# The norm factor at the opening of a second feed-forward: tokens on partitions, copied banks, and later state steps

## The chip, the core and the metric

The kernel runs on one core of a Trainium2 chip. A core has five engines, each with its own instruction queue, worked through in order: TensorE (PE in the profile; PEld is its loading of the stationary operand), VectorE (DVE), ScalarE (ACT), GpSimd (POOL) and SyncE (SP). Engines wait for one another on semaphores. Data lies in SBUF, 128 partitions wide; TensorE writes its products to PSUM, which has eight banks of 128 x 512 f32 values. The metric is the time of one execution on the device in microseconds (us), as the median of several runs.

## The reference, cut to what matters

One step of a decoder block on 512 prompt tokens and 8 sample tokens, 520 in all, with 1024 features: a feed-forward with half weight, a mixer (causal pooling heads and state-space heads), a second feed-forward with half weight, and a last norm.

```python
def _rms_norm(x, g):
    xf = x.astype(jnp.float32)
    y = xf * lax.rsqrt(jnp.mean(xf * xf, axis=-1, keepdims=True) + EPS)
    return (y * g.astype(jnp.float32)).astype(x.dtype)

def _swiglu(x, wg, wu, wd):
    return (jax.nn.silu(x @ wg) * (x @ wu)) @ wd
...
        h = h + m
        h = h + 0.5 * _swiglu(_rms_norm(h, ffn2_norm[l]), ffn2_w_gate[l], ffn2_w_up[l], ffn2_w_down[l])
```

The norm's factor is one number for each token. The kernel multiplies the products of gate and up by it, after the matrix products, since a factor of a token can be taken out of a sum over features. The mixer also gives back new recurrent states; for the 8 sample tokens each is `decay * state + x * dt * B`, 1024 rows of 128 values for each token.

## The kernel before, in words

Features lie on partitions, tokens along the free dimension, in two halves of 260 columns (`HALVES`, `HB`). The hidden width of 2816 is 22 tiles of 128. A feed-forward goes through them in groups of 6, 6, 6 and 4 (`CHUNKS`), the first group in the order 0, 3, 1, 4, 2, 5 (`order`).

Most products use a scheme with seven products in place of eight (`product`, numbers 1 to 7), each of them three products of f32 values split into a high and a low part (`mm3`, L124 to L128). Of one tile, four products add into the bank `A` (1, 6, 7, 4) and three into the pair of banks `BE` (5, 3, 2). Between the products into `A`, ScalarE copies what the bank holds to `ac` (L444). PSUM has two slots for `A`, two for `BE` (a pair each) and two single banks `ps`.

Tile 0 of the second feed-forward is different: it is computed plainly in f32 (`plain`, L317) while the mixer's last output products still run, and its gate and its up part each hold one pair of `BE`. It opens the feed-forward:

- `scales` calls `rstds` and `rstd`: TensorE multiplies the sums of squares `acc` (128 partitions x 520 tokens) by a matrix of ones, so that each partition gets the sum for every token (L171, two products of 260 columns); ScalarE takes the root out of PSUM (L172), VectorE the reciprocal (L173). The factor `r` then stands on all 128 partitions.
- `plain_out(0)` multiplies the gate's banks by `r` (VectorE, L355, two halves), applies Silu (ScalarE, L357), multiplies by `r` again (L358), and multiplies by the up part's banks (L360, two halves). L355 and L360 free the two pairs of `BE`.
- `behind`: the weights of the third tile in the order (tile 1) are prepared on VectorE only behind L355's last instruction.

Then `rest` calls `step` for each tile. Each step also calls `state` twice (or more in the last group, `catch_up`), which moves the new states of the sample tokens on by one piece: a generator of 32 items with two pieces each. An item loads rows by GpSimd's queue (L1018, L1024), scales them by four ScalarE instructions (L1044, L1045), adds them on VectorE (L1046) and stores them (L1028). Loads, scalings and stores are pinned behind what was written before them on their engine. `at_border` names the steps that leave it out. What is left at the end is run in one go before the last product of the last tile, ahead of the down products of the last group.

The order of instructions in each engine's queue is otherwise made by a planner at build time, from priorities and its own estimate of each instruction's time; `high_priority` puts a block first, and what one place of the program changes can change the order of what follows.

Of the kernel before, what the change touches and what calls it, by code (L numbers as in the profile page):

```python
# [9 lines left out]
F32 = mybir.dt.float32  # L10
F32R = mybir.dt.float32r
AF = mybir.ActivationFunctionType
ALU = mybir.AluOpType
# [3 lines left out]
P = 128  # L17
D = 1024
# [3 lines left out]
HB = NT // 2  # L22
HALVES = (slice(0, HB), slice(HB, NT))
# [38 lines left out]
def tile_trunk_step(ctx: ExitStack, tc: tile.TileContext, ins: dict, outs: dict):  # L62
    nc = tc.nc
# [20 lines left out]

    ones = cst.tile([P, P], F32, tag="ones", name="ones")
    nc.vector.memset(ones, 1.0)
    eps = cst.tile([P, 1], F32, tag="eps", name="eps")
    nc.vector.memset(eps, EPS)

# [40 lines left out]
    def ws(w, k, m=P):  # L130
        return w[:, k * m : (k + 1) * m]
# [77 lines left out]
    class Ffn:  # L209
# [3 lines left out]

        def __init__(self, nx, i, wx, gp, direct):
            self.nx, self.i, self.wx, self.gp, self.direct = nx, i, wx, gp, direct
            self.states = self.pending = self.gx = None
            self.w, self.A, self.BE, self.ac, self.g, self.tg, self.raw, self.banks, self.behind = ({} for _ in range(9))
            self.out, self.gt, self.early, self.added = {}, {}, {}, {}
            self.chunk, self.chunks, lo = {}, [], 0
            for c, n in enumerate(CHUNKS):  # L220
                fs = list(range(lo, lo + n))
                if c < PAIRED:
                    fs = [lo + q * (n // 2) + k for k in range(n // 2) for q in range(2)]
                self.chunks.append(fs)
                self.chunk.update({f: c for f in fs})
                lo += n
            self.order = [f for fs in self.chunks for f in fs]
# [77 lines left out]
        def plain(self, f, xg, j, us=(0, 1)):  # L305
            for u in us:
                if (f, u) not in self.banks:
                    n = f"P{self.i}_{f}{u}"
                    if f and u == 0:
                        bs = [ps[0].tile([P, 512], F32, tag="A", bufs=2, name=f"{n}{b}") for b in range(2)]  # L310
                    else:
                        t = ps[0].tile([P, 2, 512], F32, tag="BE", bufs=2, name=n)
                        bs = [t[:, 0], t[:, 1]]
                    self.banks[f, u] = bs
                for q in range(2):
                    for b, slot in enumerate(((0, 1), (3, 2))):
                        nc.tensor.matmul(self.banks[f, u][b][:, :HB], ws(self.raw[f][:, u], j + 4 * q), xg[:, slot[q]],  # L317
                                         start=j == q == 0, stop=j == 3 and q == 1, skip_group_check=True)
# [11 lines left out]
        def plain_mixed(self, f, xgs):  # L330
# [9 lines left out]
            for low in (False, True):  # L340
                for u in range(2):
                    w = self.w[f, u][low]
                    for j in range(n):
                        for q, b in ((0, 0), (1, 0), (1, 1)):
                            for x in (xth,) if low else (xth, xtl):
                                nc.tensor.matmul(self.banks[f, u][b][:, :HB], ws(w, j + 4 * q), x[:, j, q + b],
                                                 start=not low and x is xth and j == q == 0,
                                                 stop=low and j == n - 1 and q == 1, skip_group_check=True)

        def plain_out(self, f):  # L350
            tg = self.wx.tile([P, 2, HB], F32, tag="tg", bufs=2, name=f"tg{self.i}_{f}")
            self.tg[f] = tg
            self.g_homes(f)
            for b, hs in enumerate(HALVES):
                free = nc.vector.tensor_tensor(out=tg[:, b], in0=self.banks[f, 0][b][:, :HB], in1=self.nx[3][:, hs],  # L355
                                               op=ALU.mult)
            nc.scalar.activation(out=tg, in_=tg, func=AF.Silu)  # L357
            nc.vector.tensor_tensor(out=tg, in0=tg, in1=self.halves(self.nx[3]), op=ALU.mult)  # L358
            for b in range(2):
                nc.vector.scalar_tensor_tensor(out=self.out[f][:, b], in0=self.banks[f, 1][b][:, :HB],  # L360
                                               scalar=0.5, in1=tg[:, b], op0=ALU.mult, op1=ALU.mult)
            self.g_split(f)
            return free.ins

# [113 lines left out]
        def close(self, k):  # L478
# [4 lines left out]
            with self.first_if(k):  # L483
                self.up(k, 0, self.A[k][:, :HB])
                self.g_split(k, True)

        def scales(self):
            return rstds(self.nx, f"f{self.i}")

# [43 lines left out]
        def at_border(self, k):  # L533
            if isinstance(k, tuple):
                return k[1] in (0, 2)
            return self.chunk[k] < PAIRED and k == self.chunks[self.chunk[k]][-1]

        def state(self, k):
# [129 lines left out]
    f2 = {}  # L668
# [29 lines left out]
    f2["ffn"].states = f2["states"](f2["st"])  # L698
    next(f2["ffn"].states)
    with tc.high_priority():  # L700
        f2["ffn"].scales()
        f2["ffn"].behind[f2["ffn"].order[2]] = f2["ffn"].plain_out(0)

    res = []
# [58 lines left out]
def mixer(tc, ins, outs, e):  # L763
    nc = tc.nc
    cst, act, wp, tmp, dr, pool = (e[x] for x in ("cst", "act", "wp", "tmp", "dr", "pool"))
    ones = e["ones"]
    bank, load_unit, mm3, ws, v, rstd, rstds, vec, h, nx2, raw_tile, open_f2, fin, fill = (
        e[x] for x in ("bank", "load_unit", "mm3", "ws", "v", "rstd", "rstds", "vec", "h", "nx2", "raw_tile",
                       "open_f2", "fin", "fill"))
    xh, xl, _, r = nx2[0]  # L770
    xa = e["xa"][0]
    mp = pool("mx", "right")

    ident = cst.tile([P, P], F32, tag="ident", name="ident")
    nc.sync.dma_start(out=ident, in_=ins["ident"])
    tri = cst.tile([P, P], F32, tag="tri", name="tri")
    nc.sync.dma_start(out=tri, in_=ins["tri"])
# [544 lines left out]
```

## Time and profile before

| | |
|---|---|
| median of 3 runs | 972.12 us (971.78 to 979.32) |
| profiled execution | 970.42 us |
| its span, first to last instruction | 968.7 us |
| TensorE busy | 942.4 us, 97% |
| VectorE busy | 859.2 us, 89% |
| ScalarE busy | 694.3 us, 72% |
| GpSimd busy | 232.1 us, 24% |
| mean granted TensorE clock | 0.997 of full speed |

Times in the views count from the first instruction. A row of a timeline has start, duration, engine, line, operation, the tile written and those read, shapes and count; a bracket behind it holds the engine's idle time just before and what ended it. A row of groups has busy time and mean duration in ns, and then idle time. A row of a line's view has the shortest, the median and the longest duration in ns. A row of stretches has the length, then for PE, PEld, DVE, ACT and POOL the busy time and the number of instructions, then the granted clock, the share of DMA and GB/s. The second feed-forward's own products begin at about 619 us, and its last product ends just before 960 us.

### The profile page before, as it was taken

The numbers are of one execution on the slowest core, as the hardware profiler recorded it, in microseconds if no ns is written. First come the engines' busy times: TensorE is split into PE (matmuls) and PEld (weight loads), VectorE is DVE, ScalarE is ACT, GpSimd is POOL, SyncE is SP. The second block draws the span as 40 slices with busy tenths as digits, with TensorE's granted clock in tenths as the row PEclk, the third lists the DMA queues.
The fourth block names the chain that finished last, engine by engine and source line by source line (L and its number), as shares of the span: only waits on it lengthen the run. The fifth ranks groups of instructions, "written<-read, shape, count | busy, mean of one in ns | idle before, by whom it ended". The sixth has DMA issues, their size and how long they took to land.

```text
span 968.7 us, 20265 instructions
## 1 busy us (share of the span) xinstructions
PE 942.4 (97%) x7636; PEld 922.2 (95%) x7636; DVE 859.2 (89%) x1616; ACT 694.3 (72%) x1293; POOL 232.1 (24%) x341
## 2 busy tenths in 40 slices
PE   7999999999999999999999999999999999999995
PEld 6999999999999999989899999899999999999995
DVE  7999899989999698688989876999989999999986
ACT  8777677667767475686776556687788778887984
POOL 0111211121122000156523111122142223323430
PEclk9999999999999999999999999999999999999998
DMA  7565775675666243264598777466587668767852
GB/s 243 149 174 119 180 178 126 149 188 146 157 148 170 68 151 119 80 189 120 165 261 221 168 178 160 120 155 155 139 219 184 169 152 218 184 149 188 202 155 89
DMA packets 66739, 157.01 MB, mean 162 GB/s; under 512 B 9608, under 2 KB 22856, under 8 KB 66640
## 3 DMA queue, kind: packets, MB, share of 16 engines
q1 hardware_dynamic: 41168, 103.78, 34.0%
q0 software_dynamic: 25472, 51.92, 29.0%
q8 instruction: 60, 0.98, 0.4%
q14 instruction: 39, 0.32, 0.1%
HBM read 148.33 MB, written 7.34 MB: 161 GB/s over the span
## 4 chain that ended last, share of the span: by engine, by line
PE 86%; DVE 6%; DMA 3%; ACT 3%; issue 2%; POOL 0%; SPq 0%; DVEq 0%; ACTq 0%
PE A L128 8%; PE A L124 8%; PE A L127 8%; PE BE L128 6%; PE BE L124 6%; PE BE L127 6%; PE P L317 3%; PE wo L124 2%; PE wo L128 2%; PE wo L127 2%; PE A2d L127 2%; PE A2d L124 2%; PE A2d L128 2%; PE inz L124 2%; PE A1d L128 2%
## 5 line engine op out<-in xcount | busy, mean ns | idle before, releaser
L444 ACT COPY ac<-A 128x260 f32<-128x260 f32 x123 | 45.5, 370 | 17.0 <-PE A L128 16.6
L387 DVE TENSOR_TENSOR s<-raw 128x1024 f32<-128x1024 f32 x41 | 49.9, 1217 | 3.4 <-DMA raw<-in_w1gu 2.7
L124 PE MATMUL inz<-xh_mx,whi_inz 128*128 128x260 f32 x128 | 36.8, 287 | 1.0 <-DVE E L1122 1.0
L317 PE MATMUL P<-xg_f,raw 128*128 128x260 f32 x128 | 32.5, 407 | 5.3 <-DMA raw<-in_w1gu 5.3
L124 PE MATMUL wo<-catg,whi_wo 128*128 128x260 f32 x128 | 37.2, 290 | 0.0
L124 PE MATMUL inx<-xh_mx,whi_inx 128*128 128x260 f32 x128 | 36.4, 285 | 0.0
L128 PE MATMUL wo<-catg,wlo_wo 128*128 128x260 f32 x128 | 36.2, 283 | 0.0
L128 PE MATMUL inz<-xh_mx,wlo_inz 128*128 128x260 f32 x128 | 36.2, 283 | 0.0
L128 PE MATMUL inx<-xh_mx,wlo_inx 128*128 128x260 f32 x128 | 36.2, 283 | 0.0
L127 PE MATMUL inx<-xl_mx,whi_inx 128*128 128x260 f32 x128 | 36.1, 282 | 0.0
L127 PE MATMUL inz<-xl_mx,whi_inz 128*128 128x260 f32 x128 | 36.1, 282 | 0.0
L127 PE MATMUL wo<-catg,whi_wo 128*128 128x260 f32 x128 | 36.1, 282 | 0.0
L1028 POOL DMA_DIRECT2D out_nss<-hs x32 | 22.0, 688 | 52.1 <-DVE hs L1046 52.1
L317 PEld LDWEIGHTS P<-xg_f,raw 128*128 128x128 f32 x128 | 25.5, 204 | 9.2 <-ACT xg_f L193 5.2
L892 DVE SCALAR_TENSOR_TENSOR A<-U,h,A 128x544 f32<-128x544 f32 x36 | 28.1, 781 | 4.9 <-ACT A L890 4.6
L456 DVE TENSOR_TENSOR tg<-BE,ac 128x520 f32<-128x520 f32 x41 | 28.4, 693 | 2.8 <-PE BE L128 2.8
L466 DVE TENSOR_TENSOR tg<-tg,r_f 128x520 f32<-128x520 f32 x41 | 28.5, 695 | 2.7 <-ACT tg L464 2.6
L1146 DVE TENSOR_TENSOR h<-wo,h 128x260 f32<-128x260 f32 x48 | 19.4, 417 | 12.7 <-PE wo L128 12.7
L107 ACT CAST whi_wo<-raw_wo 128x1024 fp32r<-128x1024 f32 x12 | 12.6, 1046 | 24.7 <-issue 16.3
L998 DVE SCALAR_TENSOR_TENSOR junk<-h,cb 128x128 f32<-128x128 f32 x64 | 21.9, 343 | 9.1 <-DMA cb<-scr_bc 8.1
L464 ACT ACTIVATE tg<-tg 128x520 f32<-128x520 f32 x41 | 26.2, 639 | 3.9 <-DVE tg L463 3.9
L463 DVE TENSOR_TENSOR tg<-tg,r_f 128x520 f32<-128x520 f32 x41 | 28.4, 693 | 0.1
(1802 smaller groups left out, 4810.5 us busy)
## 6 DMA issues: line engine op xcount, KB each, us to landing
raw<-in_w2gu SPq DMA_DIRECT2D x44, 512.0 KB, 4.8
raw<-in_w1gu SPq DMA_DIRECT2D x42, 512.0 KB, 4.6
raw_1d<-in_w1d SPq DMA_DIRECT2D x24, 384.0 KB, 4.0
raw_2d<-in_w2d SPq DMA_DIRECT2D x24, 384.0 KB, 3.9
raw_wo<-in_w_out SPq DMA_DIRECT2D x12, 512.0 KB, 6.6
wlo_wo<-in_w_out POOLq DMA_DIRECT2D x12, 512.0 KB, 7.7
ab<-scr_acs SPq DMA_DIRECT2D x8, 512.0 KB, 5.7
h<-in_state_ssm SPq DMA_DIRECT2D x16, 256.0 KB, 7.4
```

Source lines behind the costliest of these rows:

```text
L124: first = nc.tensor.matmul(ps, whi, xhi, start=start, stop=False, **kw)
L127: nc.tensor.matmul(ps, whi, xlo, start=False, stop=False, **kw)
L128: nc.tensor.matmul(ps, wlo, xhi, start=False, stop=stop, **kw)
L317: nc.tensor.matmul(self.banks[f, u][b][:, :HB], ws(self.raw[f][:, u], j + 4 * q), xg[:, slot[q]], start=j == q == 0, stop=j == 3 and q == ...
L387: nc.vector.tensor_tensor(out=s1, in0=diag, in1=up0, op=ALU.add)
L444: nc.scalar.copy(keep, out[:, :HB])
L456: nc.vector.tensor_tensor(out=tg, in0=self.BE[k][:, :, :HB], in1=a, op=ALU.add)
L463: nc.vector.tensor_tensor(out=tg, in0=tg, in1=r, op=ALU.mult)
L464: nc.scalar.activation(out=tg, in_=tg, func=AF.Silu)
L466: nc.vector.tensor_tensor(out=tg, in0=tg, in1=r, op=ALU.mult)
L892: nc.vector.scalar_tensor_tensor(out=A[:, :n], in0=U[:, j : j + n], scalar=w(j), in1=A[:, :n], op0=ALU.mult, op1=ALU.add)
L1028: pin(nc.gpsimd.dma_start(out=js(outs["nss"], i), in_=t))
```

## The change

Three things change at the opening of the second feed-forward; the first feed-forward is left as it was.

1. The factor: `turned_scales` replaces `scales`. Eight products with 65 tokens of `acc` as the stationary operand and two columns of ones as the moving one put the sums on 65 partitions, 16 columns in all. Root and reciprocal work on that 65 x 16 block. Eight more products, with one column of the result spread over 128 stationary columns and a 65 x 65 identity moving, put each factor on all 128 partitions, in two banks; ScalarE copies these to `r`.
2. The plain tile: `plain_free` copies the gate's pair of banks to `tg` on ScalarE, ahead of the factor; `plain_out` copies the up pair to its home on ScalarE. The multiplications then work in SBUF, each as one instruction of 520 columns.
3. The states: `at_border` leaves out the second and third tile of the order (tiles 3 and 1).

The tile `ident` is allocated at the program's start; it is loaded where it was.

```diff
+        def gate_home(self, f):
+            if f not in self.tg:
+                self.tg[f] = self.wx.tile([P, 2, HB], F32, tag="tg", bufs=2, name=f"tg{self.i}_{f}")
+            return self.tg[f]
+
+        def plain_free(self, f):
+            nc.scalar.copy(self.gate_home(f), self.pairs[f][0][:, :, :HB])
+
         def plain_out(self, f):
-            tg = self.wx.tile([P, 2, HB], F32, tag="tg", bufs=2, name=f"tg{self.i}_{f}")
-            self.tg[f] = tg
+            tg = self.gate_home(f)
             self.g_homes(f)
-            for b, hs in enumerate(HALVES):
-                free = nc.vector.tensor_tensor(out=tg[:, b], in0=self.banks[f, 0][b][:, :HB], in1=self.nx[3][:, hs],
-                                               op=ALU.mult)
+            out, r = self.out[f], self.halves(self.nx[3])
+            if f in self.pairs:
+                nc.scalar.copy(out, self.pairs[f][1][:, :, :HB])
+                free = nc.vector.tensor_tensor(out=tg, in0=tg, in1=r, op=ALU.mult)
...
             nc.scalar.activation(out=tg, in_=tg, func=AF.Silu)
-            nc.vector.tensor_tensor(out=tg, in0=tg, in1=self.halves(self.nx[3]), op=ALU.mult)
-            for b in range(2):
-                nc.vector.scalar_tensor_tensor(out=self.out[f][:, b], in0=self.banks[f, 1][b][:, :HB],
-                                               scalar=0.5, in1=tg[:, b], op0=ALU.mult, op1=ALU.mult)
+            nc.vector.tensor_tensor(out=tg, in0=tg, in1=r, op=ALU.mult)
+            if f in self.pairs:
+                nc.vector.scalar_tensor_tensor(out=out, in0=out, scalar=0.5, in1=tg, op0=ALU.mult, op1=ALU.mult)
...
+        def turned_scales(self):
+            acc, r = self.nx[2:]
+            n, q = HB // 4, 2
+            ps = bank("psr_t")
+            for j in range(8):
+                nc.tensor.matmul(ps[:n, q * j : q * j + q], acc[:, n * j : n * j + n], ones[:, :q], start=True, stop=True,
+                                 skip_group_check=True)
+            rt = tmp.tile([P, HB], F32, tag="ta", name="rt")[:n, : 8 * q]
+            nc.scalar.activation(out=rt, in_=ps[:n, : 8 * q], func=AF.Sqrt, bias=eps[:n], scale=1.0 / D)
+            nc.vector.reciprocal(out=rt, in_=rt)
+            for b, hs in enumerate(HALVES):
+                pr = bank(f"pr_t{b}")
+                for j in range(4):
+                    c = rt[:, q * (4 * b + j) : q * (4 * b + j) + 1]
+                    nc.tensor.matmul(pr[:, n * j : n * j + n], c.to_broadcast([n, P]), ident[:n, :n], start=True,
+                                     stop=True, skip_group_check=True)
+                nc.scalar.copy(r[:, hs], pr[:, :HB])
...
         def at_border(self, k):
             if isinstance(k, tuple):
                 return k[1] in (0, 2)
+            if k in self.order[1:3]:
+                return True
             return self.chunk[k] < PAIRED and k == self.chunks[self.chunk[k]][-1]
...
     with tc.high_priority():
-        f2["ffn"].scales()
+        f2["ffn"].plain_free(0)
+        f2["ffn"].turned_scales()
         f2["ffn"].behind[f2["ffn"].order[2]] = f2["ffn"].plain_out(0)
```

More of the change, by code (lines that the diff above doesn't have):

```diff
@@ L86, in tile_trunk_step @@
     nc.vector.memset(ones, 1.0)
+    ident = cst.tile([P, P], F32, tag="ident", name="ident")
     eps = cst.tile([P, 1], F32, tag="eps", name="eps")
@@ L215, in __init__ @@
             self.nx, self.i, self.wx, self.gp, self.direct = nx, i, wx, gp, direct
+            self.pairs = {}
             self.states = self.pending = self.gx = None
@@ L313, in plain @@
                         bs = [t[:, 0], t[:, 1]]
+                        if self.i == 2:
+                            self.pairs.setdefault(f, []).append(t)
                     self.banks[f, u] = bs
@@ L348, in plain_mixed @@
                                                  stop=low and j == n - 1 and q == 1, skip_group_check=True)
+        def gate_home(self, f):
[4 more added lines that the diff above has]
+            nc.scalar.copy(self.gate_home(f), self.pairs[f][0][:, :, :HB])
         def plain_out(self, f):
-            tg = self.wx.tile([P, 2, HB], F32, tag="tg", bufs=2, name=f"tg{self.i}_{f}")
-            self.tg[f] = tg
+            tg = self.gate_home(f)
             self.g_homes(f)
-            for b, hs in enumerate(HALVES):
-                free = nc.vector.tensor_tensor(out=tg[:, b], in0=self.banks[f, 0][b][:, :HB], in1=self.nx[3][:, hs],
-                                               op=ALU.mult)
-            nc.scalar.activation(out=tg, in_=tg, func=AF.Silu)
-            nc.vector.tensor_tensor(out=tg, in0=tg, in1=self.halves(self.nx[3]), op=ALU.mult)
-            for b in range(2):
-                nc.vector.scalar_tensor_tensor(out=self.out[f][:, b], in0=self.banks[f, 1][b][:, :HB],
-                                               scalar=0.5, in1=tg[:, b], op0=ALU.mult, op1=ALU.mult)
+            out, r = self.out[f], self.halves(self.nx[3])
+            if f in self.pairs:
+                nc.scalar.copy(out, self.pairs[f][1][:, :, :HB])
+                free = nc.vector.tensor_tensor(out=tg, in0=tg, in1=r, op=ALU.mult)
+            else:
+                for b, hs in enumerate(HALVES):
+                    free = nc.vector.tensor_tensor(out=tg[:, b], in0=self.banks[f, 0][b][:, :HB],
+                                                   in1=self.nx[3][:, hs], op=ALU.mult)
+            nc.scalar.activation(out=tg, in_=tg, func=AF.Silu)
+            nc.vector.tensor_tensor(out=tg, in0=tg, in1=r, op=ALU.mult)
+            if f in self.pairs:
+                nc.vector.scalar_tensor_tensor(out=out, in0=out, scalar=0.5, in1=tg, op0=ALU.mult, op1=ALU.mult)
+            else:
+                for b in range(2):
+                    nc.vector.scalar_tensor_tensor(out=out[:, b], in0=self.banks[f, 1][b][:, :HB],
+                                                   scalar=0.5, in1=tg[:, b], op0=ALU.mult, op1=ALU.mult)
             self.g_split(f)
@@ L485, in close @@
                 self.g_split(k, True)
+        def turned_scales(self):
[8 more added lines that the diff above has]
+            nc.vector.reciprocal(out=rt, in_=rt)
+            for b, hs in enumerate(HALVES):
+                pr = bank(f"pr_t{b}")
[4 more added lines that the diff above has]
+                nc.scalar.copy(r[:, hs], pr[:, :HB])
         def scales(self):
@@ L772, in mixer @@
     mp = pool("mx", "right")
-    ident = cst.tile([P, P], F32, tag="ident", name="ident")
+    ident = e["ident"]
     nc.sync.dma_start(out=ident, in_=ins["ident"])
```

## The prediction

> **What bounds the kernel now.** I read the page first: the shares of the engines, then the chain that ended last.
>
> ```profile
> span 968.7 us, 20265 instructions
> PE 942.4 (97%) x7636; PEld 922.2 (95%) x7636; DVE 859.2 (89%) x1616; ACT 694.3 (72%) x1293; POOL 232.1 (24%) x341
> PE 86%; DVE 6%; DMA 3%; ACT 3%; issue 2%; POOL 0%; SPq 0%; DVEq 0%; ACTq 0%
> ```
>
> TensorE is busy 97% of the span and is 86% of the chain. All its idle time together is 968.7 - 942.4 = 26.3 us. So a change can gain only what it takes off TensorE's own work, plus idle time of TensorE that it closes; work given to or taken from VectorE counts only where TensorE waits for it. That makes the place of the change the next view: the timeline of TensorE from the last products of the plain tile on. An entry in brackets is idle time just before a row, with what ended it.
>
> ```profile
> 621.56 1.04 PE L171 MATMUL psr_f<-acc_f,ones 128*128 128x260 f32 x4
> 622.25 0.48 PE L124 MATMUL A<-xth_f,whi_3a 128*128 128x260 f32 x1
> 622.56 0.28 PE L127 MATMUL A<-xtl_f,whi_3a 128*128 128x260 f32 x1
> 622.68 0.28 PE L128 MATMUL A<-xth_f,wlo_3a 128*128 128x260 f32 x1
> 623.50 0.38 PE L124 MATMUL A<-xth_f,shi_3d 128*128 128x260 f32 x1 [0.54 <-ACT ac L444]
> ...
> 625.66 0.39 PE L124 MATMUL A<-xth_f,shi_3c 128*128 128x260 f32 x1 [0.47 <-ACT ac L444]
> ...
> 627.83 0.39 PE L124 MATMUL A<-xth_f,whi_3b 128*128 128x260 f32 x1 [0.47 <-ACT ac L444]
> ...
> 633.21 0.39 PE L124 MATMUL BE<-xth_f,shi_3d 128*128 128x260 f32 x1 [1.02 <-ACT ac L444]
> ...
> 637.99 0.39 PE L128 MATMUL A<-xth_f,slo_1d 128*128 128x260 f32 x1
> ...
> 659.01 0.39 PE L124 MATMUL BE<-xth_f,shi_2d 128*128 128x260 f32 x1 [0.38 <-ACT ac L444]
> ...
> 659.76 0.38 PE L128 MATMUL A<-xth_f,slo_2d 128*128 128x260 f32 x1 [0.25 <-DVE slo_2d L115]
> ```
>
> Tile 3 runs four groups of products into the one bank A, one after another, and before each of three of them waits for ScalarE to copy A away; a fourth wait is for a copy of BE. The four waits are 0.54 + 0.47 + 0.47 + 1.02 = 2.50 us. They are there because BE has only two pairs of banks and both still hold the plain tile, whose release hangs on the norm factor. Why that is late shows on VectorE and ScalarE:
>
> ```profile
> 623.63 3.41 DVE L173 RECIPROCAL r_f<-r_f 128x260 f32<-128x260 f32 x2
> 626.95 0.70 DVE L355 TENSOR_TENSOR tg<-P,r_f 128x260 f32<-128x260 f32 x2
> ...
> 630.94 0.70 DVE L358 TENSOR_TENSOR tg<-tg,r_f 128x520 f32<-128x520 f32 x1 [1.22 <-ACT tg L357]
> ...
> 632.16 0.76 DVE L360 SCALAR_TENSOR_TENSOR gx<-P,tg 128x260 f32<-128x260 f32 x2
> ```
> ```profile
> 622.34 0.84 ACT L172 ACTIVATE r_f<-psr_f,eps 128x260 f32<-128x260 f32 x2
> ...
> 627.67 0.40 ACT L1044 ACTIVATE hs<-hs,sdec 128x128 f32<-128x128 f32 x1
> ...
> 628.97 1.28 ACT L357 ACT_TABLE_LOAD   x1
> 630.27 0.64 ACT L357 ACTIVATE tg<-tg 128x520 f32<-128x520 f32 x1
> ```
>
> Two reciprocals of 3.41 us stand before L355 frees the gate's banks (627.65), and L360 frees the up half's only at 632.92. Between them the states' four scalings (627.67 on) push the table load and the Silu back, and VectorE waits 1.22 us.
>
> **The change, part by part.** First, the products that are added. The rows nearest to them are these, with the start of what follows:
>
> ```profile
> 435.11 1.09 PE L1112 MATMUL yd<-ab,xdt 128*64 128x128 f32 x16
> 436.13 0.39 PE L124 MATMUL inp<-xh_mx,whi_inp 128*128 128x260 f32 x1
> 436.36 0.28 PE L127 MATMUL inp<-xl_mx,whi_inp 128*128 128x260 f32 x1
> ...
> 370.97 1.20 PE L839 MATMUL psdv<-sel,dv 48*128 48x16 f32 x10
> 372.10 0.39 PE L124 MATMUL inbc<-xh_mx,whi_inbc 128*128 128x260 f32 x1
> ```
>
> A plain f32 product is two records (the two products of the old factor are the x4 of L171). With 64 stationary columns a record takes (436.13 - 435.11) / 16 = 0.064 us, with 128 columns and 16 moving ones (372.10 - 370.97) / 10 = 0.113 us, so the load of the stationary side sets the pace, not the moving side. The new sums are 8 products with 65 stationary columns and 2 moving: 16 records, 1.0 us by the row with 64 columns, at most 1.8 us by the other; I take 1.0. The spreading is 8 products with 128 stationary columns and 65 rows: 16 records, 1.8 us by the psdv row, at least 1.0 us; I take 1.8. The old two products leave: from 621.56 to about 622.44 (the row at 622.25 reaches its successor 0.31 us later where the pace is 0.12), 0.88 us. Coming back from f32 products costs TensorE 0.23 - 0.12 = 0.11 us at 436.13; the spreading can stand apart from the sums in one piece or two, 0.1 to 0.2 us; I take 0.2. Together 1.0 + 1.8 + 0.2 - 0.9 = **+2.1 us of TensorE work**, between 2.0 + 0.1 - 0.9 = +1.2 and 3.6 + 0.2 - 0.9 = +2.9. Nothing covers it while TensorE is the bound.
>
> [...]
>
> Second, the copies that free the banks. Two ScalarE copies of 128x520 out of the banks are added. The nearest rows are the copy of half the size and the Silu of the full size:
>
> ```profile
> L444 ACT COPY ac<-A 128x260 f32<-128x260 f32 x5 | 1.9, 375 | 4.0 <-PE A L128 4.0
> L357 ACT ACTIVATE tg<-tg 128x520 f32<-128x520 f32 x1 | 0.6, 638 | 0.0
> ```
>
> So 0.64 each (0.75 as two halves). The first can start when the plain tile's products end, near 621.7, and needs no norm factor; the second needs the slot of the sum of squares, which is free once the new sums are made, near 622.6. So the gate's pair is free about 622.4 and the up pair about 623.4, instead of 627.65 and 632.92. Tile 3 can then run in its written order, A and BE in turn, and each copy of A lies beside 12 products of another bank (12 x 0.12 = 1.4 us against 0.37). I cost this **-2.5 us**, between 0 and -2.5. ScalarE gets two copies (1.3), two more of 128x260 for the factor (0.75) and one small root; it loses the two roots (0.84). Between 618 and 640, the stretch of these rows, it sat idle 4.0 us waiting for A alone.
>
> Third, VectorE: the 3.41 us of reciprocals become one of 65x16. Nearest are a small operation of either engine:
>
> ```profile
> L854 DVE TENSOR_SCALAR dt_e<-dt_q x1: 201/201/201, 379.5 to 379.5; 128x80 f32<-128x80 f32 x1
> L1076 ACT ACTIVATE we<-we x8: 190/206/209, 418.8 to 507.9; 128x8 f32<-128x8 f32 x8
> ```
>
> 0.2 us each. But VectorE can use little of the 3.2 us: the preparation of tile 1 is queued on it behind the product that L355 makes (`behind`), and that now waits for sums (1.0), root, reciprocal, spreading (1.8) and two copies. From 621.56: 1.0 + 0.4 + 0.3 + 1.8 + 0.5 gives a factor at about 625.8 and the product done at 626.6, against 627.65. What it frees is 1.0 us there, and with the states gone the Silu follows at once, which removes the 1.22 us wait and one addition of 0.42 us: tile 1's last operand (637.99) would be ready some 2 us earlier, and TensorE arrives there at nearly the old time. Of the three small waits later (0.1 at 637.99, 0.38, 0.25) I let 0.3 go: **-0.3**, between 0 and -0.75.
>
> Fourth, the states. Two of the 32 items (two steps each for tiles 3 and 1) move to the end, ahead of the last product of tile 21. That is 8 scalings, 2 additions and the loads, one row and stores of POOL's queue. There the profile shows:
>
> ```profile
> 930.00:940.00 10.00, 9.99 (x83) 9.78 (x82) 8.22 (x16) 8.26 (x22) 3.23 (x6) 1.00 0.59 184
> 940.00:950.00 10.00, 10.00 (x86) 10.00 (x85) 8.30 (x21) 7.98 (x22) 0.55 (x1) 1.00 0.03 14
> ...
> 937.61 0.62 ACT L249 CAST gt<-tg 128x520 fp32r<-128x520 f32 x1
> ...
> 938.65 0.40 ACT L1044 ACTIVATE hs<-hs,sdec 128x128 f32<-128x128 f32 x1
> ...
> 940.68 0.55 POOL L1028 DMA_DIRECT2D out_nss<-hs  x1 [3.44 <-DVE hs L1046]
> ```
>
> An item is 4 scalings, from 938.65 to the next cast at 939.84, 1.2 us of ScalarE. Two are 2.4 us, and the twenty microseconds shown leave ScalarE 3.8 us idle, while TensorE runs on through the down products. I cost it 0; without that cover, see the third rival.
>
> **The sum.** +2.1 - 2.5 - 0.3 + 0 = -0.7 us. The profiled execution took 970.42 us (its span of 968.7 and 1.7 around it), so 969.7; the median of the runs shown is 972.12, 1.7 above it, so I forecast **971.4 us**.
>
> **The rivals.** *Slower, TensorE waits for its own factor.* TensorE takes its instructions in order. If the spreading is queued close behind the sums, it waits for drain (0.28 less the pace of 0.12), root, reciprocal and three hand-overs: 0.2 + 0.4 + 0.2 + 3 x 0.1 = 1.1 us (a hand-over: the product at 622.68 ends 622.96 and ScalarE's copy starts 623.07), and 1.2 more if the reciprocal meets one of VectorE's 1.2 us operations. It decides from the point where fewer than about ten products of tile 3 stand between. For it: the old factor was placed with only the plain tile's products before it and had priority; against it: tile 3's operands are ready and could fill the gap. 971.4 + 2.3 = 973.7 us.
>
> *Cheaper products.* The loads hide behind running products: the pace is then that of the moving side, 0.22 us for 260 columns (0.88 / 4), so 0.055 for 65 and next to nothing for 2: 16 x 0.055 = 0.9 instead of 2.8. 971.4 - 1.9 = 969.5 us. [...]
>
> *The tail.* The moved states are pinned in order. Each waits for a load:
>
> ```profile
> L1018 POOL DMA_DIRECT2D hs<-in_state_ssm x32: 538/568/899, 621.3 to 934.1; - x32
> DMA to landing us min/median/max: 2.3/3.9/6.9
> ```
>
> If two items stand ahead of the last tile's cast (937.61), ScalarE is held for 2 x 3.9 us, and TensorE's cover is 27 products of the first three outputs, 3.2 us: 4.6 us late, 971.4 + 4.6 less what ScalarE does meanwhile, about 975. For it: the last items already ran beside the down products; against it: the cast has priority.
>
> *It doesn't do what it says.* The banks are held anyway, by the next tile's operands or by the queue order: the stalls stay and the work is paid, 971.4 + 2.8 = 974.2 us.
>
> **How the numbers follow.** Chances: forecast 0.45 (own range 970.1 to 972.5: 1.2 - 2.5 - 0.75 = -2.05 and 2.9 - 2.5 = +0.4 by the ends of the terms, the stall closed), waits for the factor 0.22, cheaper products 0.12, tail 0.12, no earlier banks 0.06, and 0.03 that the planner's new order costs or gains more anywhere in the 340 us behind. The range 968.8 to 975.6 reaches from below the cheaper products to the tail. One per cent, 9.7 us, is about what a measurement of this kernel tells from no change. No case but the last reaches it: faster 0.02, within 0.94, slower 0.04.
>
> **What would show it.** Right: records of the sums near 0.065 us and of the spreading near 0.11; no row of tile 3 in TensorE's timeline that waits for a copy of A; BE written right after the first group of A; the Silu straight behind its product. Wrong: an idle entry before the spreading that names the reciprocal or the root; new waits for ScalarE's copies, now that four more stand in its queue; idle time of TensorE between 930 and 945. The forecast falls too if the new order opens wider waits at the later borders between groups of tiles, of which this is one today:
>
> ```profile
> PE BE2d L124 <- ACT shi_2d_0c L107: 0.9, 1, 0.9
> ```

## The result, and the profile after

The changed kernel takes 979.18 us (median of 22 runs, 973.07 to 985.49), the kernel before, run beside it, 975.73 us (22 runs, 969.72 to 980.74). The medians differ by 3.4 us; the ratio of the runs, estimated with its 95% interval, is 1.0051 (1.0031 to 1.0071): slower by half a per cent, 5.0 us, where no change to speak of was forecast. Its profiled execution took 976.3 us. The page of the changed kernel begins so (engines, then the shares of the chain that ended last):

```profile
span 974.5 us, 20318 instructions
PE 945.7 (97%) x7664; PEld 925.5 (95%) x7664; DVE 855.3 (88%) x1613; ACT 695.3 (71%) x1296; POOL 232.2 (24%) x341
PE 80%; DVE 7%; DMA 7%; ACT 3%; issue 2%; POOL 1%; SPq 0%; DVEq 0%; ACTq 0%; POOLq 0%
```

TensorE's idle time is now 974.5 - 945.7 = 28.8 us against 26.3, and it is busy 3.3 us longer. To see where, I cut the span on TensorE at three instructions that both kernels have: the first product for the norm factor's sums; the first product with `shi_2d_0c` (685.38 before, 688.47 after); and the first with `whi_21a` (920.03 and 923.12). **Opening**, **middle** and **tail** are the stretches from each to the next, the tail up to the span's end.

| | sums start at | opening | middle | tail |
|---|---|---|---|---|
| before | 621.56 | 63.82 | 234.65 | 48.67 |
| after | 622.99 | 65.48 | 234.65 | 51.38 |
| difference | 1.43 | 1.66 | 0.00 | 2.71 |

Ahead of the opening TensorE's records show the same instructions in the same order, but for a few records that either trace lacks, so I put the 1.43 us there down to the execution, not to the change. In a second profile of the changed kernel (e6) the sums start at 623.43, and in a kernel that differs from the one before only in its states (e9) at 625.29. The change costs 1.66 us where it is made and 2.71 us at the end: 4.4 us in this pair of profiles, beside 5.0 us in the timed runs.

TensorE's timeline of the opening after the change (start, duration, instruction, idle time before it in brackets):

```profile
622.99 1.05 PE L511 MATMUL psr_t<-ones,acc_f 128*65 128x2 f32 x16
623.90 0.37 PE L125 MATMUL A<-xth_f,whi_3a 128*128 128x260 f32 x1
624.11 0.28 PE L125 MATMUL BE<-xth_f,shi_3c 128*128 128x260 f32 x1
...
626.05 0.39 PE L125 MATMUL A<-xth_f,shi_3d 128*128 128x260 f32 x1
...
627.59 1.90 PE L520 MATMUL pr_t<-ident,rt 65*128 65x65 f32 x16
629.29 0.37 PE L125 MATMUL BE<-xth_f,shi_3d 128*128 128x260 f32 x1
...
639.05 0.39 PE L125 MATMUL A<-xth_f,shi_1d 128*128 128x260 f32 x1 [1.04 <-ACT shi_1d L108]
...
641.10 0.41 PE L129 MATMUL A<-xth_f,slo_1d 128*128 128x260 f32 x1 [1.27 <-DVE slo_1d L116]
...
641.51 0.42 PE L128 MATMUL A<-xtl_f,shi_1d 128*128 128x260 f32 x1
641.73 0.42 PE L129 MATMUL A<-xth_f,slo_1d 128*128 128x260 f32 x1
...
644.76 0.29 PE L125 MATMUL BE<-xth_f,shi_1d 128*128 128x260 f32 x1
```

The sums take 623.90 - 622.99 = 0.91 us, the spreading 629.29 - 627.59 = 1.70. `BE` is written straight behind the first products into `A`, and no row of tile 3 has an idle entry; only the one at 626.05 starts 0.39 us behind the row before it, where the pace is 0.12, just as ScalarE's copy of `A` ends (626.00). But tile 1 now waits twice, 1.04 + 1.27 us, nearly as long as the four waits that went. And behind those waits a product starts 0.22 us after the last one (641.51, 641.73) where the pace elsewhere is 0.12. The view of stretches says why (length, busy time and count for PE, PEld, DVE, ACT, POOL, granted clock, DMA share, GB/s):

```profile
638.00:641.20 3.20, 0.89 (x6) 0.68 (x5) 3.20 (x5) 1.81 (x4) 0.86 (x1) 1.00 0.88 221
641.20:644.80 3.60, 3.60 (x18) 3.60 (x19) 3.39 (x8) 0.90 (x2) 0.00 (x0) 0.53 0.75 197
644.80:648.00 3.20, 3.20 (x28) 3.20 (x28) 2.32 (x4) 2.42 (x4) 0.00 (x0) 1.00 0.00 0
```

In 3.2 us TensorE was busy for 0.89; in the 3.6 us that follow its granted clock is 0.53. Why the operands of tile 1 are late shows on VectorE, where they are prepared, and on ScalarE. VectorE after the change:

```profile
625.05 0.24 DVE L515 RECIPROCAL rt<-rt 65x16 f32<-65x16 f32 x1
629.93 0.70 DVE L368 TENSOR_TENSOR tg<-tg,r_f 128x520 f32<-128x520 f32 x1 [4.64 <-ACT r_f L522]
...
639.82 1.22 DVE L116 TENSOR_TENSOR slo_1d<-s,shi_1d 128x1024 fp32r<-128x1024 f32 x1
```

ScalarE after the change:

```profile
629.52 0.38 ACT L522 COPY r_f<-pr_t 128x260 f32<-128x260 f32 x1 [0.52 <-PE pr_t L520]
629.92 1.28 ACT L373 ACT_TABLE_LOAD   x1
631.21 0.64 ACT L373 ACTIVATE tg<-tg 128x520 f32<-128x520 f32 x1
...
636.48 1.05 ACT L108 CAST whi_4a<-raw 128x1024 fp32r<-128x1024 f32 x1 [0.93 <-PE A L128]
637.43 0.63 ACT L112 ACTIVATE wlo_4a<-raw 128x512 fp32r<-128x512 f32 x1
637.97 1.03 ACT L108 CAST shi_1d<-s 128x1024 fp32r<-128x1024 f32 x1
```

The reciprocal starts 0.70 us behind the end of the root, since VectorE is still at work on another operation (L208, 1.24 us from 623.89), and is done at 625.29. But TensorE spreads it only at 627.59, behind three groups of tile 3, where the planner has put it. VectorE, in order, stands idle for 4.64 us before L368, and everything for tile 1 is queued behind L368. On ScalarE the casts of tile 4 then stand ahead of that of `shi_1d`.

The tail, TensorE after the change:

```profile
938.46 0.39 PE L125 MATMUL dh<-gt,shi_2d 128*128 128x260 f32 x1 [0.42 <-ACT shi_2d L108]
...
957.95 0.60 PE L780 MATMUL psl<-acc_last,ones 128*128 128x260 f32 x2
...
960.66 0.60 PE L780 MATMUL psl<-acc_last,ones 128*128 128x260 f32 x2
962.42 0.71 PE L780 MATMUL psl<-sq_last,ones 128*128 128x260 f32 x2 [1.16 <-ACT sq_last L764]
963.57 0.71 PE L780 MATMUL psl<-sq_last,ones 128*128 128x260 f32 x2 [0.44 <-ACT sq_last L764]
```

and before it:

```profile
951.00 0.60 PE L740 MATMUL psl<-acc_last,ones 128*128 128x260 f32 x2
...
956.70 0.60 PE L740 MATMUL psl<-acc_last,ones 128*128 128x260 f32 x2
957.42 0.71 PE L740 MATMUL psl<-sq_last,ones 128*128 128x260 f32 x2
```

`psl` is the last norm's sum, one for each half of the tokens. Before, the first half's stood 5.70 us ahead of the second's, and its root and reciprocals ran beside TensorE's last down products. After, it stands 2.71 us ahead. TensorE waits for nothing there; only its place in the queue is later. So the reciprocals of the first half fall behind TensorE's last down product. VectorE before, and then after:

```profile
953.79 0.97 DVE L747 RECIPROCAL r_last<-r_last 128x130 f32<-128x130 f32 x1 [0.77 <-ACT r_last L744]
```
```profile
960.61 0.97 DVE L787 RECIPROCAL r_last<-r_last 128x130 f32<-128x130 f32 x1 [1.65 <-ACT r_last L784]
```

From the last down product (956.58 and 960.54) to the span's end it was 12.12 us and is 13.96: 1.84 of the 2.71 us. The other 0.87 us lie before it. There ScalarE waits 1.59 us for the load of a state, its cast of `shi_2d` is late, and the idle entry of 0.42 us at 938.46 follows. Whether this is the work of the moved states is a question for e1:

```profile
936.09 0.40 ACT L1084 ACTIVATE hs<-hs,sdec 128x128 f32<-128x128 f32 x1 [1.59 <-DMA hs<-in_state_ssm]
...
937.80 0.60 ACT L108 CAST shi_2d<-raw_2d 128x512 fp32r<-128x512 f32 x1
```

### The profile page after: what moved, and what is told of

Same layout as the page of the kernel before. It is cut to its first block, busy times and chain, and to the rows that moved or that the text cites. A ratio compares the mean times of both kernels' runs of the same rounds, so it can differ in the third digit from the quotient of the medians.

```text
span 974.5 us, 20318 instructions
## 1 busy us (share of the span) xinstructions
PE 945.7 (97%) x7664; PEld 925.5 (95%) x7664; DVE 855.3 (88%) x1613; ACT 695.3 (71%) x1296; POOL 232.2 (24%) x341
## 4 chain that ended last, share of the span: by engine, by line
PE 80%; DVE 7%; DMA 7%; ACT 3%; issue 2%; POOL 1%; SPq 0%; DVEq 0%; ACTq 0%; POOLq 0%
PE A L129 8%; PE A L125 8%; PE A L128 8%; PE BE L129 6%; PE BE L128 6%; PE BE L125 6%; PE P L321 3%; PE wo L125 2%; PE wo L129 2%; PE wo L128 2%; DMA cb<-scr_bc 2%; PE A2d L128 2%; PE A2d L125 2%; PE A2d L129 2%; PE A1d L129 2%
```

## The experiments

Theory: the opening gave its gain back through a late factor and a lowered clock, and the rest is the price of the states at the end. Rivals: the added products themselves cost more than their records show; the copies or the new factor hurt by taking ScalarE; the end is slower for reasons of its own. The stretches of every kernel, from one profile each, and the ratio to the kernel before in timed runs:

| | opening | middle | tail | ratio, 95% interval |
|---|---|---|---|---|
| before | 63.82 | 234.65 | 48.67 | |
| after | 65.48 | 234.65 | 51.38 | 1.0051, 1.0031 to 1.0071 |
| e1_states_back | 63.88 | 234.69 | 49.76 | 1.0013, 0.9977 to 1.0049 |
| e2_states_alone | 61.52 | 234.65 | 51.28 | 1.0021, 0.9992 to 1.0051 |
| e3_copies_alone | 63.62 | 234.71 | 48.98 | 1.0011, 0.9976 to 1.0045 |
| e10_factor_alone | 62.84 | 234.71 | 49.34 | one run |
| e5_spread_early | 61.53 | 234.69 | 51.67 | 1.0011, 0.9980 to 1.0041 |
| e6_after_again | 65.47 | 234.69 | 51.81 | one run |
| e7_kept_busy | 63.95 | 234.69 | 52.55 | 1.0015, 0.9988 to 1.0042 |
| e8_early_caught_up | 61.54 | 235.72 | 49.42 | 0.9973, 0.9948 to 0.9998 |
| e9_states_caught_up | 61.53 | 235.33 | 48.65 | 0.9969, 0.9943 to 0.9995 |

Runs of one kernel spread by some 10 us, so the timed ratios separate only the ends of this list. The stretches are read from single profiles, and some show a kernel's fastest execution (e2's took 972.19 us, where its median is 978.34); the changed kernel's opening came out at 65.48 and 65.47 in two.

### The states as before: e1

Against the changed kernel:

```diff
-            if k in self.order[1:3]:
-                return True
```

> The changed kernel with the states' steps of tiles 3 and 1 put back (part three undone). Measured in the profile are two stretches of TensorE: the opening, from the first sums of the norm factor to the first product with shi_2d_0c (63.82 us before, 65.48 changed), and the tail, from the first product with whi_21a to the end of the span (48.67 before, 51.38 changed). Theory one, two places: the opening's +1.66 comes of the late factor and the added products, the tail's +2.71 of the two moved items. Then the tail is back at 48.7 (within 0.4) and the opening stays at 65 to 67; +1.5 to +3 us against the kernel before. Rival, only the added products count and the tail's difference is variation from run to run: the tail comes out anywhere between 48 and 52, with the opening at 65.5.

Measured: 975.01 us (10 runs) beside 974.12 (31). The tail is 49.76, 1.6 us less than after the change, and the opening 63.88; 48.7 and 65 to 67 were expected. The last norm's sums stand 5.69 us apart again, and the time behind the last down product is back at 12.08 us: that 1.84 us of the tail's loss hangs on the moved states. The stretch before that product is not shorter, though: it is 1.13 us longer than in the kernel before, where the changed kernel was 0.87 longer, with a wait of the same kind:

```profile
935.61 0.39 PE L125 MATMUL dh<-gt,shi_2d 128*128 128x260 f32 x1 [0.34 <-ACT shi_2d L108]
```

So the 0.87 us are not shown to come of the moved states. New factor and copies together leave the opening where it was before (63.82): they pay for their own products and gain no more. The factor is as late here as after the change (L368 starts 6.95 us behind the sums, 6.94 there), but the planner has put the cast of `shi_1d` ahead of those of tile 4:

```profile
635.26 1.06 ACT L108 CAST shi_1d<-s 128x1024 fp32r<-128x1024 f32 x1
```

It starts 13.49 us behind the sums instead of 14.98, the waits at tile 1 are 0.82 and 0.56 us with twelve products between them, and the products behind them start 0.12 us apart (638.86 to 639.82). With the late factor and the copies, leaving out the states cost 1.6 us of the opening; alone it gains, as e2 shows.

### The states alone: e2

Against the kernel before:

```diff
         def at_border(self, k):
             if isinstance(k, tuple):
                 return k[1] in (0, 2)
+            if k in self.order[1:3]:
+                return True
```

> The kernel before with only the states' steps of tiles 3 and 1 left out (part three alone). Theory one: the tail is 51.4 (within 0.4), as in the changed kernel, and the opening is 62.5 to 63.8, since the Silu no longer stands behind four scalings; +1.5 to +2.7 us. Rival, the tail's difference is variation: tail 48.7, +0 or a little faster.

Measured: 978.34 us (10 runs) beside 974.12. The opening falls to 61.52, 2.3 us below before and 1 us below the range expected: with no scalings in ScalarE's queue the plain tile's Silu comes sooner (7.50 us behind the sums instead of 8.71), and the waits at 633.21, 659.01 and 659.76 of the kernel before are gone; only the three for copies of `A` are left. The tail is 51.28, that of the changed kernel. Its rows on TensorE:

```profile
953.80 0.60 PE L742 MATMUL psl<-acc_last,ones 128*128 128x260 f32 x2
956.51 0.60 PE L742 MATMUL psl<-acc_last,ones 128*128 128x260 f32 x2
958.28 0.71 PE L742 MATMUL psl<-sq_last,ones 128*128 128x260 f32 x2 [1.17 <-ACT sq_last L726]
```

The two sums stand 2.71 us apart, as after the change. So the moved states alone bring the later sum and the 1.84 us behind it, with no new factor and no copies (here 14.01 us behind the last down product; the stretch before it is 0.72 us longer than in the kernel before). And they alone bring more gain in the opening than the other two parts.

### The copies alone: e3

Against the changed kernel, beside the two lines of e1:

```diff
-        f2["ffn"].turned_scales()
+        f2["ffn"].scales()
```

> The changed kernel with the factor made as before (roots and reciprocals of 128x260) and the states where they were: part two alone. Theory one: the four waits of tile 3 (2.50 us) go without the 1.7 us of added products, but VectorE still does 3.4 us of reciprocals and tile 1's preparation stays queued behind them, so part of the time comes back as waits on tile 1: opening 61.5 to 63.5, tail 48.7, -0.3 to -2 us. Rival, the waits only move (TensorE ends up waiting the same for tile 1): opening 63.8.

Measured: 975.62 us (10 runs) beside 974.12; the opening is 63.62, 0.2 us less than before. The list of TensorE's waits between 618 and 662 us (instruction, what it waited for, total, count, longest):

```profile
PE A L129 <- DVE slo_1d L116: 1.7, 1, 1.7
PE BE L129 <- DVE slo_1c L116: 1.4, 1, 1.4
PE A L125 <- ACT shi_1d L108: 0.2, 1, 0.2
```

The waits of tile 3 are gone, and as much has come up at tile 1, since the two reciprocals (3.41 us together) still stand ahead of tile 1's operands on VectorE. Copying the banks out moves the stall by one tile; by itself it removes nothing.

### The factor alone: e10

Against the changed kernel, beside the two lines of e1:

```diff
-                        if self.i == 2:
-                            self.pairs.setdefault(f, []).append(t)
...
-        f2["ffn"].plain_free(0)
```

> The changed kernel without the copies of the banks and with the states where they were: part one alone. Theory one: the sums and the spreading cost 2.6 us of TensorE in place of 0.7, the four waits for ScalarE's copies stay, since the gate's banks are still freed by a product with the factor: opening 64.5 to 66, tail 48.7 to 49.8. Rival, the reciprocal's 3.2 us on VectorE are worth more than the products: opening 62.5 to 63.8.

Measured: 973.38 us beside 971.51, one run each; the opening is 62.84, 1.0 us less than before, where 64.5 to 66 was expected. Of the waits for copies of `A` one is left:

```profile
PE A L125 <- ACT ac L461: 0.5, 1, 0.5
```

So in this profile the new factor is worth more than its products cost, when the banks are freed by the products with it as before; with the copies beside it (e1, 63.88) that gain is gone. That the parts don't add up is shown by one profile each. The spreading stands 3.5 us behind the sums here and 4.6 in e1; that this takes the 1.0 us is likely and was not tried by itself.

### Spreading the factor sooner: e5

Against the changed kernel, tile 3's later products are issued behind the spreading (`spread` is its last product):

```diff
-                    nc.tensor.matmul(pr[:, n * j : n * j + n], c.to_broadcast([n, P]), ident[:n, :n], start=True,
-                                     stop=True, skip_group_check=True)
+                    self.spread = nc.tensor.matmul(pr[:, n * j : n * j + n], c.to_broadcast([n, P]), ident[:n, :n],
+                                                   start=True, stop=True, skip_group_check=True).ins
...
-                self.product(k, p)
+                early = self.i == 2 and k == self.order[1] and p != 5
+                with tc.issue_after(self.spread) if early else nullcontext():
+                    self.product(k, p)
```

> The changed kernel with the spreading products ahead of tile 3's second group of products in TensorE's queue (its later products are queued behind them), so some 1.5 us earlier. Theory one, tile 1's preparation waits on VectorE for the factor, and TensorE's 1.04 and 1.27 us waits are that: the factor's product on VectorE starts at 5.2 to 5.6 us after the sums instead of 6.9, the two waits shrink by 1.3 to 2 us, the opening is 63.5 to 64.2; the tail stays at 51.4; +2.5 to +3.5 us. Rival, the waits come of ScalarE's order (the cast of shi_1d behind two others): the opening stays at 65.2 to 65.7.

Measured: 977.86 us (10 runs) beside 974.12. The sums start at 625.31 in this profile, the spreading 2.8 us behind them instead of 4.6, and the product L368 5.1 us behind them instead of 6.9:

```profile
628.10 1.90 PE L520 MATMUL pr_t<-ident,rt 65*128 65x65 f32 x16
```
```profile
630.45 0.70 DVE L368 TENSOR_TENSOR tg<-tg,r_f 128x520 f32<-128x520 f32 x1 [2.83 <-ACT r_f L522]
```

Of the two waits at tile 1 one of 0.62 us is left (in e8, which has the same edit, the products behind that wait start 0.12 us apart, 637.25 to 639.66), and the opening is 61.53: 3.95 us less than after the change, with the same products, and less than the 63.5 to 64.2 expected. The edit names only the place of the products, but the planner's order of what follows changed with it. On ScalarE the cast of `shi_1d` now stands ahead of those of tile 4:

```profile
637.33 1.06 ACT L108 CAST shi_1d<-s 128x1024 fp32r<-128x1024 f32 x1
```

It starts 12.02 us behind the sums instead of 14.98, 3.0 us sooner, where L368 is 1.8 us sooner. So the place of the spreading and the order that followed from it were worth 3.95 us together. The rival, ScalarE's order, is not excluded as a part of it: in e1 that order came with a factor as late as after the change, and the opening was 63.88. The tail is as bad as before this edit (51.67).

### The changed kernel once more, and with TensorE kept busy: e6 and e7

> The changed kernel itself, a second look. Its first profile shows the granted clock at 0.53 from 641.2 to 644.8, behind two waits of 1.04 and 1.27 us, so that 17 products took 0.22 us each instead of 0.12, 1.7 us in all. Theory two: that follows from the waits, so it is there again in the same place, the opening is 65.5 (within 0.4) and the tail 51.4 (within 0.5). Rival, the clock fell by chance: full pace here, opening 63.8.

The changed kernel again, in a second profile, 977.18 us: the same waits of 1.04 and 1.27 us, and behind them the same fall:

```profile
638.00:641.20 3.20, 1.23 (x8) 0.81 (x7) 3.20 (x5) 2.25 (x4) 0.86 (x1) 1.00 0.95 236
641.20:644.80 3.60, 3.26 (x18) 3.26 (x19) 3.60 (x9) 0.90 (x2) 0.00 (x0) 0.65 0.82 211
```

In e7, 22 products into a bank that nobody reads stand where the waits were, against the changed kernel:

```diff
-                self.product(k, p)
+                fill = None
+                if self.i == 2 and k == self.order[2] and p == 6:
+                    wb, (wh, _) = bank("warm"), self.w[k][1][0]
+                    for q in range(22):
+                        fill = nc.tensor.matmul(wb[:, :HB], ws(wh, q % 4), self.nx[0][:, q % 4, 0], start=True, stop=True,
+                                                skip_group_check=True)
+                        tc.keep_in_program_order(fill)
+                with tc.issue_after(fill.ins) if fill is not None else nullcontext():
+                    self.product(k, p)
```

> The changed kernel with 22 more products (2.65 us) between tile 1's second and third group, into a bank that nobody reads, so that TensorE computes while it would wait for tile 1's operands. Theory two, the waits let the clock fall: with the waits filled the clock stays at 1.0, the 1.7 us are saved, and the added products cost little since they lie where TensorE waited (2.6 us with the cost of stopping and starting): opening 63.6 to 64.4 against 65.48, the granted clock 1.0 throughout 635 to 650. Rival, the products run slowly there for another cause (SBUF or PSUM ports): the opening is 65.5 to 68.

Measured: 976.37 us (10 runs) beside 976.44 (29). Timeline and stretches:

```profile
638.93 2.81 PE L564 MATMUL warm<-xth_f,whi_1a 128*128 128x260 f32 x22
```
```profile
638.00:641.20 3.20, 3.20 (x29) 3.20 (x28) 3.20 (x6) 2.90 (x5) 0.87 (x1) 1.00 0.75 152
641.20:644.80 3.60, 3.60 (x30) 3.39 (x29) 3.60 (x7) 1.00 (x2) 0.00 (x0) 1.00 0.98 270
```

The clock stays at 1.00 and the opening is 63.95: 22 x 0.12 = 2.65 us of work more, and 1.5 us less time. The waits that the filler covers account for it only with the slow products gone too: 65.48 + 2.65 - 2.6 for the waits - 1.5 for the slow products = 64.0. So here the fall of the clock came with the idle time of TensorE, and is a cost of its own, 1.5 us, beside the waits.

### The states caught up early: e8 and e9

The last question was whether the tail's loss can be had back while the opening's gain is kept. In both kernels tiles 3 and 1 leave out their states' steps, and two tiles of the next group, 9 and 7, take two more each. e8 is the changed kernel with this and the edit of e5; e9 is the kernel before with this and the edit of e2, neither factor nor copies.

```diff
-                if p == 3 or self.catch_up(k):
+                if p == 3 or self.catch_up(k) or self.i == 2 and k in self.chunks[1][1:3] and p in (5, 7):
```

> The changed kernel with the spreading ahead of tile 3's second group (as in e5_spread_early) and the four left-out pieces of the states made up in tiles 9 and 7, two more in each, not at the end. Theory one, the tail's cost is that of two items at the end: tail 48.7 to 49.8, opening 61.5, the stretch between 234.6 to 235.4; -1.2 to -2.3 us against the kernel before by these stretches. Rival, the tail's cost comes of the planner's order whatever the place of the items: tail 51.4.

> The kernel before with the states' steps of tiles 3 and 1 left out and made up in tiles 9 and 7: neither new factor nor copies. Theory one: opening 61.5 as in e2_states_alone, tail 48.7 to 49.8, between 234.6 to 235.4; -1.2 to -2.3 us by these stretches, so that the factor and the copies add nothing. Rival, the items cost the same in tiles 9 and 7 as in 3 and 1: between 236.5 to 237, +0 us.

Measured: e8 973.01 us and e9 972.84 (12 runs each) beside 976.44 (29), both a little faster than the kernel before, with intervals that just leave out 1. By the stretches of single profiles it is 0.5 and 1.6 us. TensorE's rows at the end, first e8, then e9:

```profile
950.33 0.60 PE L782 MATMUL psl<-acc_last,ones 128*128 128x260 f32 x2
956.03 0.60 PE L782 MATMUL psl<-acc_last,ones 128*128 128x260 f32 x2
```
```profile
953.12 0.60 PE L742 MATMUL psl<-acc_last,ones 128*128 128x260 f32 x2
958.82 0.60 PE L742 MATMUL psl<-acc_last,ones 128*128 128x260 f32 x2
```

The sums stand 5.70 us apart again, and the tail is 49.42 and 48.65. The steps that were added cost 1.1 and 0.7 us in the middle (e8 lies outside its range there, 234.6 to 235.4). The opening is 61.54 and 61.53, the same with the new factor and the copies as without them. So beside the states' move the factor and the copies added nothing, even with the spreading sooner, and e9 has the gain with three lines.

## Why the prediction was wrong, step by step

The forecast was -0.7 us, with a range of 968.8 to 975.6 that reached 3.5 us above the median then known; the change cost 4.4 us by the profiles, 5.0 by the runs. Of the 7.8 us between 971.4 and 979.18, 3.6 are not the change's: the forecast started from a median of 3 runs, 972.12, where 22 runs of the kernel before gave 975.73. The terms of the sum, with what they measured, in us of TensorE's time (a wait is counted here as the time between two starts less the pace of 0.12, and includes the first product behind it, which is 0.10 longer, as from 623.50 to 623.72 before the change):

| term | predicted | measured |
|---|---|---|
| sums, spreading, old products gone | +2.1 | 0.91 + 1.70 - 0.69 = +1.9 |
| tile 3's four waits | -2.5 | -3.55, with 0.38 back at 626.05 |
| later small waits | -0.3 | -1.6 |
| new waits at tile 1 | 0 | +2.8 |
| lowered clock | not in the sum | +1.5 |
| the tail, under "states at the end" | 0 | +2.7 |

Unrounded, the rows of the opening add up to 1.5 of its 1.66 us.

**The products** held: 0.057 us for a record of the sums and 0.106 for the spreading, against 0.064 and 0.113. The rival of cheaper products, with 0.9 us for all of them, is out.

**The copies that free the banks** did what was said: `BE` is written right behind the first group of `A`, and no idle entry of tile 3 names a copy of `A` (0.38 us of such a wait, without an entry, is left at 626.05). By themselves they gain nothing (e3). The waits were worth more than their idle entries: 0.82 us lie between the starts at 622.68 and 623.50 before the change, 0.70 more than the pace, where the entry says 0.54, and 0.10 more goes on the next row.

**The step that failed in the opening** is the third, "a factor at about 625.8 and the product done at 626.6, against 627.65" (its terms add up to 625.56). It was done at 630.63, 629.2 when the 1.43 us ahead of the opening are taken off: 1.6 us later than the old one instead of 1.0 sooner. Root and reciprocal took no longer than they were priced at (0.27 and 0.24 us), though VectorE began the reciprocal 0.70 us late; the spreading then stood 2.30 us behind the reciprocal's end, its place in TensorE's queue, which no term of the sum had. The first rival had looked at that place from one side only: TensorE waiting for its factor, if the spreading came too soon. It came too late, TensorE waited for nothing there, and VectorE's queue carried the delay to tile 1. The conclusion that "TensorE arrives there at nearly the old time" as the operand fell with it. That the place costs this, together with the order of casts that followed from it, is shown by e5, which wins 3.95 us. The two are not separated: in e1 the factor is as late, the cast of `shi_1d` comes ahead of tile 4's, and the opening is 63.88.

**The clock** was a column of the stretches and no term of the sum. That the new waits also slowed what follows is shown by e7: its clock is 1.00 from 641.20 to 644.80, where the changed kernel's is 0.53 and 0.65.

**The Silu straight behind its product** was right, and worth more than its term: e2 gains 2.3 us in the opening by the states alone, where -0.3 was put down for all that follows the factor. Some 1.3 us of this is the wait at 633.21, which the sum had under the copies and which goes without them.

**The states**, "I cost it 0", failed. The third rival had the right place, and its mechanism (ScalarE held by a load ahead of a cast) is seen before the last down product, where 0.87 us were lost; but e1 loses 1.13 there with the states in their old place, so the cause of this part stays open. The larger part, 1.84, was in no case: the last norm's first sum slid back in TensorE's queue. That the moved states cause it is shown by e2, which has it with the states alone, and by e1 and e9, which undo it; by which of its estimates the planner moves the sum was not looked into.

**The chances** gave 0.04 to a loss of over 1%, and a loss of 0.5% lies among the cases within 1%; but the range was too narrow: its bounds let each case come alone, and here a loss in the opening that was no case came together with one at the end, above a kernel whose own median lay 3.6 us higher.

## What to carry to other kernels

When a short chain crosses from one engine to another and back, price the place of each link in its queue, too late as well as too soon, and look at what is queued behind the consumer: the new operation's duration was the smaller part here. Work that is put off comes due at the end, and where the end is a chain of its own (here the last norm), its price is read there and not from idle shares of the engines. Split a change into its parts before keeping it: here one part of three alone gained most in the opening, what it gained depended on the other two, and one other edit kept the gain without them.

## What was not expected of the hardware

The granted clock fell to about half (0.53 and 0.65 over 3.6 us, in two profiles; 0.22 us a product instead of 0.12) with no long gap: two waits of 1.04 and 1.27 us with four products between them came before it, 0.89 us of work in 3.2 (1.23 in the second profile). In the first profile the slow products reach from 641.3 to 644.8, 3.4 us, and then the clock is whole again (1.00 from 644.80 to 648.00); in the second it is 0.86 over that stretch. In e3, waits of 1.37, 0.19 and 1.67 us within 5.5 us left the clock at full speed (1.00 from 634.80 to 642.40), so the sum of idle time alone does not decide.

The time of a run goes with its mean granted clock: 1.3 us for each 0.001 over the 22 runs of the changed kernel (0.988 to 0.995, 0.991 in the mean), 1.4 and 1.6 over the two sets of 29 and 31 runs of the kernel before (0.994 and 0.995 in the mean). e2 has 0.992 in the mean too, with the clock at 1.00 from 638.00 to 644.80 of its profile. That the same waits of 1 to 2 us lower the clock in some executions and not in others would account for it, but no run shows it.
